# A second chunk pair with seven products in the second and seventh up pairs of each channel mixer

## The chip, the cores and the metric

One core of a Trainium2 chip runs the whole program. The metric is device time in microseconds of one execution; the time given for a kernel is the median of its runs. Engines are named as in the profile: PE is TensorE, DVE is VectorE, ACT is ScalarE, POOL is GpSimd, SP is the queue that issues most loads.

## What is computed

A decoder trunk of two layers over 256 tokens of width 2048, in float32. Layer 0 mixes tokens with gated linear attention, layer 1 with forgetting attention; both also attend to 256 memory tokens. After each mixer comes the channel mixer, which the change touches:

```python
def causal_dwconv(u, w, b):                     # width 3, along the tokens
    up = jnp.pad(u, ((0, 0), (CONV_WIDTH - 1, 0), (0, 0)))
    return w[0] * up[:, 0:s_] + w[1] * up[:, 1:s_ + 1] + w[2] * up[:, 2:s_ + 2] + b

def conv_ffn(h, w_up, conv_w, conv_b, w_down):  # FFN_HIDDEN = 5632
    u = causal_dwconv(h @ w_up, conv_w, conv_b)
    a, val = split_cols(u, [FFN_HIDDEN, FFN_HIDDEN])
    return (jax.nn.silu(a) * val) @ w_down
...
    h = rmsnorm(x, norm_ffn[i])
    x = x + conv_ffn(h, ffn_w_up[i], ffn_conv_w[i], ffn_conv_b[i], ffn_w_down[i])
```

## The kernel before

**Products in parts.** Weights come from memory in float32, in units of 128 rows by up to 1024 columns. Each unit is split: ScalarE casts it to the matmul's shorter format (`whi`), VectorE subtracts that from the original (`wlo`). Activations are held in the same two parts. A product then takes three matmuls: high by high, low by high, high by low.

**The channel mixer.** Its 44 hidden blocks of 128 channels are worked through in groups of four, called up pairs here and named by their first block j = 0, 4, 8, ... 40: eleven a layer. One up pair multiplies all 256 tokens (two blocks of 128) by 1024 columns, in 16 chunks of 128 rows of the weights, one unit each. For an ordinary chunk there are four products (two token blocks by two column halves), twelve matmuls of 128 x 512. Blocks 0 to 15, 16 to 31 and 32 to 43 form three parts (`PARTS`). After the up pairs of a part and one pair of the next, two `down_pair` calls multiply the finished blocks by the down weights. So pairs 0, 4, 8, 12, 16 come first, then two down pairs, then 20, 24, 28, 32, two down pairs, 36, 40, and the rest of the down projection.

**Seven products.** `pair_steps` can take two neighbouring chunks as the two halves of a 2 x 2 block product, with seven products instead of eight: 21 matmuls instead of 24. For that it needs sums of the activations (a tile `usum` or `dsum`, made by `input_sums` and `token_sums`) and sums of the weights, which VectorE makes in place (L425 to L428). It also splits four pieces where two chunks need two:

```python
w1 = split_more(ra[:, :512], 512)
w2 = split_more(rb, 1024)
# four differences on VectorE, L425 to L428, over ra and rb
w3 = split_more(ra, 1024)
w4 = split_more(rb, 1024)
```

`raw2` has two buffers, so a second such chunk pair in one up pair loads its units once the first pair's are used up. Eight banks gather the products. When the last chunk pair of seven is done, `early` combines four of them, on ScalarE (L1464, L1465, L1471) and VectorE (L1466 to L1469); at the end of the up pair `late` (L1475) adds the others. Before the change every up pair has chunks 6 and 7 taken so (`SEVEN_UP`), and pairs 20 and 36, the first after each two down pairs, have chunks 11 and 12 as well (`SEVEN_MORE`).

**Convolution.** An up pair's results are transposed on VectorE (L1427), sent to memory and back by GpSimd's queue, and then become taps on ScalarE (L1376), tap sums on VectorE (L1383), a silu (L1389) and a gated product (L1396, L513, L514). `drive` gives this work out chunk by chunk during the next up pair, from its eighth chunk on, and it runs on into the pair behind that.

**Order.** A scheduler fixes each engine's order of instructions when the program is built; splits have a raised priority, and taps are tied behind the last cast issued. Buffers `raw`, `whi` and `wlo` are four deep, so weights are split about three chunks ahead.

Of the kernel before, what the change touches and what calls it, by code (L numbers as in the profile page):

```python
# [35 lines left out]
SEVEN_DOWN = (4, 10)  # L36
SEVEN_MORE = 11
# [108 lines left out]
def _trunk(ctx: ExitStack, tc: tile.TileContext, xt, xtok, memt, wp, wgu, gns, gfin, cnv, par, msk, out):  # L146
# [310 lines left out]
    def token_sums(r, dst):  # L457

        t = r.rearrange("p s (b n) -> p (s b) n", b=2)
        a11, a21, a12, a22 = (t[:, n, :] for n in range(4))  # L460
        V.tensor_tensor(a22, a21, a22, ALU.add)
        V.tensor_tensor(a21, a11, a21, ALU.subtract)
        V.tensor_tensor(a11, a22, a11, ALU.subtract)
        V.tensor_tensor(a12, a12, a11, ALU.subtract)
        halves([dst[:, part] for part in range(2)], t)
# [846 lines left out]
    def down_pair(l, p, f, src, sums, flip, pool, temps, then=None):  # L1312

        def early(bank):
            t0, t1 = temps()
            S.activation(t0, bank["p1"], AF.Copy)
            add_to(f)(0, t0)
            V.tensor_tensor(t0, bank["p6"], t0, ALU.add)
            V.tensor_tensor(t1, bank["p7"], t0, ALU.add)
            add_to(f)(1, t1)  # L1320
            add_to(f + 1)(1, t1)
            add_to(f + 1)(1, bank["p5"])
            V.tensor_tensor(t0, bank["p5"], t0, ALU.add)
            add_to(f + 1)(0, t0)

        def late(b, h, a):
            add_to(f + h)(b, a)
            if then is not None:
                then(f + h, b)

        return pair_steps(where["down", l, p, f], src, sums, flip, pool, early, late)
# [26 lines left out]
    def ffn(l, nx, h, m, ys, zs, landing, then, pool, temps, last=None, spare=None):  # L1358
        with tc.tile_pool(name=f"ffn{l}", bufs=1) as fp:
# [8 lines left out]
            def held(name, i):  # L1368
                return fp.tile([P, 2, 4, P], F32R, name=name, tag=f"{name}{i}")
# [36 lines left out]
            def input_sums(k, tag="usum", at=None):  # L1406

                r = fp.tile([P, 2, T], F32, name="cv", tag="cv")
                for s in range(2):
                    V.tensor_tensor(r[:, s, :], h[k + s][:, 0, :].bitcast(F32), h[k + s][:, 1, :].bitcast(F32), ALU.add)  # L1410
                t = held(tag, k if at is None else at)
                token_sums(r, t)
                return t
# [42 lines left out]
            def up_pair(j, more={}):  # L1456

                count[2] += 1
                turns = [turn(j + 2 * h_, 8) for h_ in range(2)]
                u = {}  # L1460

                def early(bank):
                    u.update({(b, h_): temps(2 * b + h_) for b in range(2) for h_ in range(2)})
                    S.activation(u[0, 1], bank["p1"], AF.Copy)  # L1464
                    S.activation(u[0, 0], bank["p1"], AF.Copy, scale=scale(0))  # L1465
                    V.tensor_tensor(u[0, 1], bank["p6"], u[0, 1], ALU.add)  # L1466
                    V.tensor_tensor(u[1, 0], bank["p7"], u[0, 1], ALU.add)
                    V.tensor_tensor(u[0, 1], bank["p5"], u[0, 1], ALU.add)
                    V.tensor_tensor(u[1, 1], bank["p5"], u[1, 0], ALU.add)  # L1469
                    for b, h_ in ((0, 1), (1, 0), (1, 1)):  # L1470
                        S.activation(u[b, h_], u[b, h_], AF.Copy, scale=scale(b))  # L1471

                def late(b, h_, a):
                    with tc.issue_after(turned_last[0].ins) if h_ and not b else nullcontext():
                        V.scalar_tensor_tensor(u[b, h_], a, scale(b), u[b, h_], ALU.mult, ALU.add)  # L1475
                    turns[h_](b, u[b, h_])

                return pair_steps(where["up", l, j], h, {**up_sums, **more}, count[2] % 2, pool, early, late)
# [6 lines left out]
            def drive(steps, share=1.3):  # L1485
                for _ in steps:
                    tick(share)
# [2 lines left out]
            for k in up_pair(0):  # L1490
                first(k)
            done = 4
            more = {}
            for p, (lo, hi) in enumerate(PARTS[:-1]):
                while done < hi + 4:
                    drive(up_pair(done, more))
                    more = {}
                    done += 4
                src = [m[c % RING] for c in range(lo, hi)]
                for f in (0, 2):  # L1500
                    count[2] += 1
                    drive(down_pair(l, p, f, src, {c - lo: t for c, t in sums.items() if f}, count[2] % 2, pool,
                                    lambda: (temps(0), temps(1))))
                sums.clear()
                more = {SEVEN_MORE: input_sums(SEVEN_MORE, "dsum", SEVEN_DOWN[0])}
            lo, hi = PARTS[-1]
            while done < hi:
                drive(up_pair(done, more), 1.3 if done + 4 < hi else 1.7)
                more = {}
                done += 4  # L1510
            p = len(PARTS) - 1
# [83 lines left out]
    with tc.tile_pool(name="stash", bufs=1) as st:  # L1595
        vt = st.tile([P, 2, FOX_H * HD], F32, name="fvt")
        turned3 = vt.rearrange("p b t -> p (b t)").rearrange("p (f q k b j) -> p f q k b j", f=3, q=4, k=4, b=2)
        turned3 = [turned3[:, f] for f in range(3)]

        with tc.tile_pool(name="turn1", bufs=1) as tp:  # L1600
            n2, then = preparing("kv", bufB, tp, dram, turned3, "raw2", nc.gpsimd)
            ys = [const.tile([P, 4, 4, 2, 32], F32, name="yu", tag=tag) for tag in ("mk0", "mv0")]
            fixed = [vt.rearrange("p b t -> p (b t)")[:, 2048 + 512 * i : 2560 + 512 * i] for i in range(2)]

            def temps(i):
                return fixed[i] if i < 2 else tp.tile([P, 512], F32, name="temp", tag=f"temp{i}")

            more = []
            for t, tag in ((mk, "mk1"), (mv, "mv1")):
                parked.append(dram.tile([P, 4 * T], F32, name="park" + tag, tag="park" + tag, bufs=1))  # L1610
                nc.gpsimd.dma_start(parked[-1], t[1].rearrange("p a b -> p (a b)"))
                more.append(const.tile([P, 2, 2, T], F32R, name="more" + tag, tag=tag))
            ffn(0, n, bufB, bufA + [t[:, i] for t in more for i in range(2)], ys, turned3, ys, then, tp, temps)
        fox(n2, vt, turned3)
# [9 lines left out]
    with tc.tile_pool(name="store", bufs=1) as op:  # L1624
# [55 lines left out]
        then.begin = begin  # L1680
        more = [op.tile([P, 2, T], F32R, name=f"more{i}") for i in range(RING - KC)]
        ffn(1, n, bufA, bufB + more, ys, zs, zs, then, op, temps, last, spare)


# [69 lines left out]
```

## Time and profile before

| | |
|---|---|
| three timed runs | 2239.08, 2239.31, 2239.30 us; median 2239.3 us |
| the profiled execution | 2237.85 us |
| its span, first to last instruction | 2236.1 us |
| granted TensorE clock, mean | 0.997 |
| matmuls | 10323 |

Busy time of an engine is given in microseconds and as a share of the span. Idle time stands in brackets or behind a bar, with the engine or transfer that ended it. A group names line, engine and operation, then out<-in by tile names.

### The profile page before, as it was taken

To read this page: it belongs to the slowest core of one execution; us is meant where nothing else is said; L and a number is where in the kernel's file an instruction comes from. 1 tells how busy PE (TensorE), PEld (TensorE's weight loads), DVE (VectorE), ACT (ScalarE), POOL (GpSimd) and SP (SyncE) were. 2 spreads that over 40 slices of the span, in tenths; PEclk is the share of its full clock that TensorE was granted. 3 is DMA by queue.
4 is the path that set the end of the run, shared out by engine and by line. 5 is a ranking of instruction groups with operands and counts; after the bars stand their busy time and mean duration, and the time that the engine had idled before them with its cause. 6 is when DMAs were issued, how large, how long until landed. Compare 5 with 4: busy or idle time off the path is not lost.

```text
span 2236.1 us, 30039 instructions
## 1 busy us (share of the span) xinstructions
PE 2212.4 (99%) x10323; PEld 1853.4 (83%) x10323; DVE 1781.5 (80%) x2638; ACT 1419.7 (63%) x2255; POOL 137.2 (6%) x259
## 2 busy tenths in 40 slices
PE   9999999999999999999999999999999999999998
PEld 7888888888788888888877998888878888888886
DVE  7768977688887889888868559668898788978876
ACT  6655664556786567665665455455787647676466
POOL 0000000001100001100111000000100000110010
PEclk9999999999999999999999999999999999999999
DMA  9867567777677567766677767777677756765674
GB/s 347 252 220 226 195 187 245 245 244 240 216 248 251 197 212 254 228 220 215 229 245 252 217 199 247 221 243 240 222 231 240 246 196 233 259 231 208 223 240 160
DMA packets 165633, 515.47 MB, mean 231 GB/s; under 512 B 20700, under 2 KB 41832, under 8 KB 165480
## 3 DMA queue, kind: packets, MB, share of 16 engines
q1 hardware_dynamic: 148200, 460.32, 62.1%
q0 software_dynamic: 16704, 52.44, 7.6%
q8 instruction: 81, 1.33, 0.2%
q10 hardware_dynamic: 576, 0.79, 0.1%
q14 instruction: 72, 0.59, 0.1%
HBM read 469.68 MB, written 43.79 MB: 230 GB/s over the span
## 4 chain that ended last, share of the span: by engine, by line
PE 91%; ACT 4%; issue 2%; DMA 2%; DVE 0%; POOL 0%; SPq 0%; ACTq 0%; DVEq 0%; POOLq 0%
PE acc L400 27%; PE acc L333 24%; PE ps_s L400 14%; PE ps_o L400 7%; PE ps_t L400 7%; PE acc L305 3%; PE acc L260 3%; PE ps_s L333 2%; ACT tap L1376 2%; PE acc L258 1%; DMA fvt<-far 1%; ACT whi L229 1%; PE acc L361 1%; DMA yzu<-far 1%; PE ps_s L1007 0%
## 5 line engine op out<-in xcount | busy, mean ns | idle before, releaser
L230 DVE TENSOR_TENSOR wlo<-raw,whi 128x1024 fp32r<-128x1024 f32 (+4 forms) x739 | 874.9, 1195 | 296.7 <-ACT whi L229 270.2
L229 ACT ACTIVATE whi<-raw 128x1024 fp32r<-128x1024 f32 (+4 forms) x739 | 761.4, 1037 | 448.2 <-PE acc L333 165.8
L333 PE MATMUL acc<-whi,B 128*128 128x512 f32 (+3 forms) x1248 | 294.9, 371 | 8.7 <-ACT B L524 8.7
L333 PEld LDWEIGHTS acc<-whi,B 128*128 128x128 f32 x1248 | 228.1, 189 | 37.5 <-ACT B L524 9.1
L375 ACT ACTIVATE whi<-raw 128x1024 fp32r<-128x1024 f32 (+1 forms) x136 | 129.8, 955 | 196.6 <-PE acc L400 78.3
L400 PE MATMUL acc<-whi,B 128*128 128x512 f32 x794 | 203.3, 390 | 1.4 <-ACT whi L229 1.3
L376 DVE TENSOR_TENSOR wlo<-raw,whi 128x1024 fp32r<-128x1024 f32 (+1 forms) x136 | 148.0, 1089 | 71.0 <-ACT whi L375 62.4
L400 PE MATMUL acc<-whi,mix 128*128 128x512 f32 x754 | 192.6, 390 | 0.9 <-ACT whi L229 0.7
L400 PEld LDWEIGHTS acc<-whi,B 128*128 128x128 f32 x794 | 148.5, 188 | 34.6 <-ACT whi L229 3.8
L400 PEld LDWEIGHTS acc<-whi,mix 128*128 128x128 f32 x754 | 141.3, 188 | 32.3 <-ACT whi L229 2.6
L333 PE MATMUL acc<-wlo,B 128*128 128x512 f32 (+3 forms) x624 | 159.8, 370 | 0.0
L1376 ACT ACTIVATE tap<-yzu,cw 128x256 f32<-128x256 f32 x264 | 124.5, 530 | 6.2 <-DMA yzu<-far 6.0
L1376 ACT ACTIVATE tap<-fvt,cw 128x256 f32<-128x256 f32 x264 | 124.4, 530 | 4.9 <-DMA fvt<-far 4.9
L333 PEld LDWEIGHTS acc<-wlo,B 128*128 128x128 f32 x624 | 114.9, 188 | 14.6
L1383 DVE TENSOR_TENSOR tap<-tap,tap 128x1024 f32<-128x1024 f32 x88 | 106.9, 1214 | 18.8 <-ACT tap L1376 18.8
L400 PE MATMUL acc<-wlo,B 128*128 128x512 f32 x397 | 112.3, 390 | 0.0
L400 PE MATMUL ps_s<-whi,mix 128*128 128x512 f32 x394 | 107.3, 389 | 0.0
L400 PE MATMUL acc<-wlo,mix 128*128 128x512 f32 x377 | 106.6, 390 | 0.0
L400 PE MATMUL ps_s<-whi,B 128*128 128x512 f32 x342 | 94.2, 389 | 0.0
L400 PEld LDWEIGHTS acc<-wlo,B 128*128 128x128 f32 x397 | 74.4, 188 | 15.9 <-DVE wlo L230 0.5
L400 PEld LDWEIGHTS ps_s<-whi,mix 128*128 128x128 f32 x394 | 74.0, 188 | 15.7
L400 PEld LDWEIGHTS acc<-wlo,mix 128*128 128x128 f32 x377 | 70.6, 188 | 15.2 <-DVE wlo L230 0.5
(490 smaller groups left out, 3756.0 us busy)
## 6 DMA issues: line engine op xcount, KB each, us to landing
raw<-wp SPq DMA_DIRECT2D x743, 512.0 KB, 4.5
fvt<-far POOLq DMA_DIRECT2D x100, 128.0 KB, 5.4
raw<-wp SPq DMA_DIRECT2D x32, 384.0 KB, 3.4
far<-yu POOLq DMA_DIRECT2D x22, 512.0 KB, 5.6
far<-yzu POOLq DMA_DIRECT2D x22, 512.0 KB, 5.8
yzu<-far POOLq DMA_DIRECT2D x88, 128.0 KB, 5.0
raw<-wp SPq DMA_DIRECT2D x24, 388.0 KB, 3.7
x<-xtok SPq DMA_DIRECT2D x8, 512.0 KB, 5.7
```

Of the source, the lines that this page charges most:

```text
L229: casts.append(S.activation(hi[:, s], raw[:, s], AF.Copy))
L230: lows.append(V.tensor_tensor(lo[:, s], raw[:, s], hi[:, s].bitcast(F32), ALU.subtract))
L258: mm = TE.matmul(acc[p][c][:, :T], w[:, s], both[:, 0, :], start=False, stop=end and j == 3)
L260: mm = TE.matmul(acc[p][c], w[:, s], both, start=u == j == 0, stop=end and j == 3)
L305: mm = TE.matmul(acc[b][:, :n], src[kcs[j] - base][:, part, b * P : (b + 1) * P], w, start=u == 0 and low == part == j == 0, stop=u == end ...
L333: mm = TE.matmul(acc[b][:, :n], src[kc - base][:, part, b * P : (b + 1) * P], ready[low][:, j * n : (j + 1) * n], start=i == low == part = ...
L361: mm = TE.matmul(acc[b][:, :n], src[kc - base][:, part, b * P : (b + 1) * P], w, start=i == low == part == j == 0, stop=i == end and low = ...
L375: casts.append(S.activation(hi[:, :n], src, AF.Copy))
L376: lows.append(V.tensor_tensor(lo[:, :n], src, hi[:, :n].bitcast(F32), ALU.subtract))
L400: r = TE.matmul(bank[name], x, w, start=name not in begun, stop=last)
L1376: S.activation(by_run(taps[i][:, s, c, i:]), zs[slot][:, :, 2 * c + s], AF.Copy if i else AF.Identity, bias=0.0 if i else w[3], scale=w[2 ...
L1383: V.tensor_tensor(taps[0], taps[0], taps[n][:, :, :, :T], ALU.add)
```

## The change

`more` names the additional chunk pair of the next up pair. The change makes its sums already after up pair 0, in the tile that block sums number 4 use later (`dsum4`), and lets pair 4 take them. In the second part it keeps them for one pair longer, so that pair 24 has them beside pair 20. Pair 36 is as before. Four up pairs of a layer then take chunks 11 and 12 with seven products instead of two. Lines behind 1493 move down by one.

```diff
             for k in up_pair(0):
                 first(k)
             done = 4
-            more = {}
+            more = {SEVEN_MORE: input_sums(SEVEN_MORE, "dsum", SEVEN_DOWN[0])}
             for p, (lo, hi) in enumerate(PARTS[:-1]):
                 while done < hi + 4:
                     drive(up_pair(done, more))
-                    more = {}
+                    if not p or done != lo + 4:
+                        more = {}
                     done += 4
```

## The prediction

> **What bounds the kernel now.** I read the page's busy times and chain first, then a table of stretches, one per pair of weight panels, then TensorE's waits, then VectorE's queue in order of time.
>
> ```profile
> span 2236.1 us, 30039 instructions
> ...
> PE 2212.4 (99%) x10323; PEld 1853.4 (83%) x10323; DVE 1781.5 (80%) x2638; ACT 1419.7 (63%) x2255; POOL 137.2 (6%) x259
> ...
> PE 91%; ACT 4%; issue 2%; DMA 2%; DVE 0%; POOL 0%; SPq 0%; ACTq 0%; DVEq 0%; POOLq 0%
> ```
>
> TensorE (PE) is the chain: 91% of it. Whatever takes matmuls away pays, as long as nothing makes TensorE wait instead. The profiled execution took 2237.85 us, 1.75 us around its span; the median of the three timed runs, 2239.3 us, is 1.45 us more. I add the change to the span and carry both differences along.
>
> The next rows are whole pairs: up pair 4, up pair 8, up pair 20 (already with two chunk pairs of seven products), up pairs 24 and 28, all of the first layer. Columns: stretch, length, then busy time of PE, weight loads, VectorE (DVE), ScalarE (ACT), GpSimd.
>
> ```profile
> core 0: us, PE busy (x) PEld busy (x) DVE busy (x) ACT busy (x) POOL busy (x), PEclk, DMA share, GB/s
> 500.50:543.40 42.90, 42.90 (x190) 35.46 (x189) 33.81 (x39) 31.83 (x50) 5.44 (x10) 1.00 0.72 233
> 543.40:587.20 43.80, 43.41 (x190) 35.32 (x189) 38.42 (x49) 33.48 (x54) 5.47 (x10) 1.00 0.70 234
> 760.00:802.40 42.40, 42.40 (x187) 34.92 (x186) 33.70 (x38) 22.94 (x25) 0.00 (x0) 1.00 0.57 194
> 802.40:845.50 43.10, 43.10 (x190) 35.32 (x189) 34.98 (x43) 32.13 (x51) 5.50 (x10) 1.00 0.72 233
> 845.50:888.60 43.10, 43.10 (x190) 35.38 (x190) 38.44 (x46) 33.02 (x54) 5.47 (x10) 1.00 0.76 244
> ```
>
> Pair 20 gives the pace: 42.40 / 187 = 0.227 us a matmul. It runs without a wait because the down pairs ahead of it left no convolution work: ScalarE has 22.94 us to do. Pairs 4 and 24, which the change edits, carry 31.83 and 32.13. Only pairs 8, 24 and 28 here make TensorE wait, and they wait for splits of weights:
>
> ```profile
> PEld acc L400 <- ACT whi L229: 0.5, 2, 0.2
> PEld ps_o L400 <- ACT whi L229: 0.2, 1, 0.2
> ...
> PEld acc L400 <- ACT whi L229: 0.8, 1, 0.8
> PEld acc L400 <- DVE wlo L230: 0.3, 1, 0.3
> ```
>
> The first two lines are pairs 24 and 28 together, the last two pairs 4 and 8. So the slack behind TensorE is nearly spent there, and the quarters of pair 24 and the first of pair 28 show where:
>
> ```profile
> 813.10:823.80 10.70, 10.70 (x48) 8.63 (x47) 5.21 (x7) 6.43 (x11) 2.17 (x4) 1.00 0.59 155
> 823.80:834.50 10.70, 10.70 (x48) 8.72 (x48) 10.50 (x11) 10.70 (x18) 0.00 (x0) 1.00 0.53 177
> 834.50:845.40 10.90, 10.90 (x50) 9.03 (x49) 9.53 (x15) 10.81 (x21) 0.00 (x0) 1.00 0.79 263
> 845.50:856.20 10.70, 10.70 (x49) 8.83 (x48) 10.70 (x14) 4.98 (x7) 2.66 (x5) 1.00 0.88 326
> ```
>
> VectorE idles half of the second quarter and then hardly at all. The idle quarter cannot be borrowed: the convolution's taps, which feed the later sums, come back from memory only at its end.
>
> ```profile
> 820.28 2.52 ACT L1376 ACTIVATE tap<-fvt,cw 128x256 f32<-128x256 f32 x6 [0.90 <-DMA fvt<-far]
> ```
>
> **The change part by part.** *Matmuls.* In four pairs (4 and 24 of both layers) chunks 11 and 12 take 7 x 3 products instead of 2 x 12: 12 matmuls fewer in all, 12 x 0.227 = 2.7 us, on the path. The Trainium skill, "TensorE: Matmul & The Clock Gate", section "Wait — 56ns, not 53.3ns?", gives 215.7 ns for a warm matmul of 512; by that estimate the saving would be 2.6 us, and the row's 227 ns decides.
>
> *Splits.* Instead of two casts and two low parts there are four of each, one of them half as wide, and four differences (L425 to L428) on VectorE.
>
> ```profile
> L376 DVE TENSOR_TENSOR wlo<-raw,whi 128x1024 fp32r<-128x1024 f32 x15 | 18.4, 1224 | 9.6 <-ACT whi L375 9.4
> L427 DVE TENSOR_TENSOR raw<-raw,raw 128x512 f32<-128x512 f32 x5 | 3.5, 691 | 0.1
> L376 DVE TENSOR_TENSOR wlo<-raw,whi 128x512 fp32r<-128x512 f32 x5 | 3.4, 687 | 2.3 <-PE ps_t L400 1.4 <-ACT whi L375 1.0
> L375 ACT ACTIVATE whi<-raw 128x1024 fp32r<-128x1024 f32 x15 | 15.9, 1061 | 21.2 <-PE ps_t L400 11.2 <-PE acc L400 7.5 <-DVE raw L426 2.4
> L375 ACT ACTIVATE whi<-raw 128x512 fp32r<-128x512 f32 x5 | 3.2, 634 | 6.9 <-PE ps_t L400 3.3 <-PE acc L400 1.7 <-DVE wlo L230 1.6
> ```
>
> Added per pair: 2 x 1.22 of low parts less the two replaced, so one wide, one half (1.22 + 0.69) and 4 x 0.69, 4.7 us of VectorE; neighbours overlap a little (two low parts take 2.35 us in a row quoted below, not 2.44), so 4.5 us of its queue. ScalarE gets 1.06 + 0.63 = 1.7 us, and new waits: its third and fourth casts want VectorE's differences. Behind them stand the early sums and the casts of chunks 13 and 14, and TensorE waits for all three.
>
> *Moved.* The early sums of products (L1464 to L1469) follow the last chunk pair of seven, so they go from chunk 6 to chunk 11, behind the second split and before the convolution's second half. *Loads.* The second chunk pair's two loads wait on SP for the first's buffers, with the later weight loads queued behind them. In pair 20 this is already so:
>
> ```profile
> 775.54 3.04 SPq L419 DMA_DIRECT2D raw<-wp  x2
> ...
> raw<-wp SPq DMA_DIRECT2D x743, 512.0 KB, 4.5
> ```
>
> They go out 15.5 to 18.6 us into a pair and land 4.5 us later, by 23.1; TensorE needs them after 129 matmuls, at 29. I count nothing; were the cover gone, they would cost what they are late. GpSimd's queue keeps its order. *Input sums.* Once a layer, during pair 0: seven more VectorE steps, none wider than 512, so at most 7 x 0.69 = 4.8 us. Pair 0's last quarter has 10.80 - 5.71 = 5.1 us free, so I count nothing; with that cover gone it would cost up to those 4.8 us a layer.
>
> ```profile
> 489.60:500.40 10.80, 10.80 (x49) 8.97 (x48) 5.71 (x6) 3.83 (x4) 0.00 (x0) 1.00 0.77 254
> ```
>
> **VectorE's queue from pair 24 into pair 28.** The built program shows the new order. From the first tap sum (L1383) to the last split of pair 28's own seven products it holds what it held, plus 4.5 us, plus the four early sums (4 x 0.6, 0.69 less the overlap; before they ran ahead of it). The old stretch and its idle time:
>
> ```profile
> 830.15 1.22 DVE L1383 TENSOR_TENSOR tap<-tap,tap 128x1024 f32<-128x1024 f32 x1
> 831.29 2.35 DVE L230 TENSOR_TENSOR wlo<-raw,whi 128x1024 fp32r<-128x1024 f32 x2
> ...
> 838.20 1.23 DVE L230 TENSOR_TENSOR wlo<-raw,whi 128x1024 fp32r<-128x1024 f32 x1 [0.55 <-ACT whi L229]
> 839.95 1.23 DVE L230 TENSOR_TENSOR wlo<-raw,whi 128x1024 fp32r<-128x1024 f32 x1 [0.52 <-ACT whi L229]
> ...
> 843.02 1.23 DVE L230 TENSOR_TENSOR wlo<-raw,whi 128x1024 fp32r<-128x1024 f32 x1 [0.19 <-ACT whi L229]
> ...
> 865.35 1.23 DVE L376 TENSOR_TENSOR wlo<-raw,whi 128x1024 fp32r<-128x1024 f32 x1 [1.66 <-ACT whi L375]
> ```
>
> It ran from 830.15 to 866.6, 36.4 us with 2.9 idle: 33.5 of work. With 6.9 more and all idle gone it is 40.4; it starts about 1.1 sooner, the early sums no longer being ahead of it, so it ends at 829.05 + 40.4 = 869.5, 2.9 us later than before. TensorE needs that last split at once, so it is late by as much, though it has 0.7 us less to do. One 0.2 us wait after it goes, since casts now stand ahead of taps: net +2.7 us. The floor comes from whole stretches (823.8 on is chunk 8's low part):
>
> ```profile
> 823.80:866.60 42.80, 39.51 (x50) 1.00 0.72 240
> 1877.90:1921.20 43.30, 39.62 (x50) 1.00 0.69 240
> 520.80:564.30 43.50, 37.96 (x45) 1.00 0.69 233
> 1576.20:1619.00 42.80, 37.97 (x45) 1.00 0.69 234
> ```
>
> 39.51 + 4.5 = 44.0 does not fit into 42.80: at least +1.2. If all idle stays, +4.5. In the second layer the same stretch has room for 0.4 more: +2.2 (0.8 to 4.5). Pairs 4 and 8 have more slack: 37.96 + 4.5 is 1.0 below the first room and, in the second layer, 37.97 + 4.5 is 0.3 below. Laid out the same way the queue ends 1.1 later there, since the new splits wait for each other, but pair 8's old wait of 0.8, for a cast behind eight taps, goes, because casts move ahead of them: I take +0.3, and +0.9 in the second layer, where the room is 0.7 smaller (each from -1.0, the saving and that wait in part, to +4.0).
>
> Sum, the saving inside each term: 2.7 + 2.2 + 0.3 + 0.9 = 6.1, rounded to +6.0 us. Span 2242.1, profiled time 2243.9, median 2245.3 us. Without the saving the waits would be 8.7.
>
> **The rivals.** *The saving holds (not slower).* The convolution work slips behind without TensorE noticing: its results are wanted only by a down pair much later. For: pair 20 has two chunk pairs and no wait. Against: low parts stand in the same queue as tap sums, and 44.0 does not fit 42.8. It decides if the queue lets splits pass. 2239.3 - 2.7 = 2236.6; chance 0.12. *Idle time all used.* Each stretch at its floor: 1.2 + 0.8 in pairs 24 and 28, -0.7 each in 4 and 8, where only the saving is left: +0.6, 2239.9; chance 0.24. *ScalarE ties the knot.* In pairs 8 and 28 the new order puts the early sums' first two ScalarE steps ahead of the third cast, in pair 28 a copy of chunk sums too; the early sums wait for TensorE, and TensorE for the cast. For: VectorE must finish that copy's input first, late as it is. Against: there the old cast waited for VectorE anyway. It decides if the cast starts later than VectorE's second difference allows. Three half-wide ScalarE steps of 0.6 in each following pair, on top of the forecast: 4 x 1.8 = 7.2, 2252.5; chance 0.13. *The clock falls.*
>
> ```profile
> 1173.00:1184.00 11.00, 5.12 (x14) 4.08 (x15) 8.97 (x34) 4.53 (x13) 4.52 (x9) 0.54 1.03 330
> ```
>
> Between the layers TensorE is idle for some 9 us and the granted clock drops to 0.54 for the next stretch; here, if the waits lump into a single long one, about 10 us at half speed costs 5 us more in each of pairs 28: 2255.3; chance 0.03. The Trainium skill's page above, Part 1, lets the clock drop after an idle window of about 3.4 us; the up pairs' waits so far, 0.8 at most, leave it at 1.00, which agrees. That the change does not do what it says is out: the built order shows the new products.
>
> **How the numbers follow.** The forecast has 0.48. The range 2238.0 to 2252.5 leaves out the first rival and the last, 0.15. About 0.2%, 4.5 us, is what a measurement of this kernel can tell from no change. Faster by that, below 2234.8, needs the whole saving and most old waits gone: 0.02, out of the first rival. Within it lie the rest of the first two rivals, 0.34, and 0.02 of the forecast's own low end: 0.36. Slower, above 2243.8: the rest, 0.62.
>
> **What would show it.** Right: 10311 matmuls; pair 24 no shorter than its 43.1, more likely 44; VectorE without idle time from the second split to pair 28's seven; pair 28 some 2 us longer with TensorE waiting for L376 or L375; pair 8 without its old waits. Wrong: pairs 24 and 28 at 42.4 and 43.0, or VectorE idle at 860.

## The result, and the profile after

The changed kernel takes 2251.64 us (median of six runs, 2250.76 to 2254.24), the kernel before, run beside it, 2239.19 us (six runs, 2237.99 to 2241.40). The ratio is 1.0057, 95% interval 1.0047 to 1.0068: 12.4 us slower, twice the +6.0 that was forecast. The profiled execution took 2254.01 us, its span 16.1 us more than that of before. A second profiled execution of the same kernel (below) took 2251.61 us, the median.

The page of the changed kernel:

```profile
span 2252.2 us, 30067 instructions
...
PE 2217.4 (98%) x10311; PEld 1850.3 (82%) x10311; DVE 1798.5 (80%) x2676; ACT 1425.4 (63%) x2265; POOL 137.1 (6%) x259
...
PE 83%; issue 7%; DMA 3%; ACT 3%; DVE 3%; POOL 1%; SPq 0%; ACTq 0%; DVEq 0%; POOLq 0%
```

There are 12 matmuls fewer, as the change promises, and the share of TensorE in the chain falls from 91% to 83%. Most of that went to "issue" (2% to 7%), time for which the profile shows no wait, and the second execution has 89%, so what TensorE waits for is better read from the stretches. The first layer's up pairs 4, 8, 24, 28 and 32 of the changed kernel, as stretches:

```profile
core 0: us, PE busy (x) PEld busy (x) DVE busy (x) ACT busy (x) POOL busy (x), PEclk, DMA share, GB/s
500.30:543.70 43.40, 43.29 (x188) 34.65 (x187) 34.96 (x41) 29.26 (x44) 5.45 (x10) 1.00 0.67 215
543.70:590.20 46.50, 44.76 (x190) 36.40 (x189) 41.00 (x51) 37.18 (x63) 5.46 (x10) 0.96 0.77 245
805.30:848.60 43.30, 43.22 (x187) 34.57 (x186) 34.94 (x41) 28.38 (x43) 5.50 (x10) 1.00 0.68 220
848.60:893.60 45.00, 43.26 (x191) 35.32 (x190) 40.64 (x53) 36.87 (x62) 5.47 (x10) 1.00 0.73 244
893.60:937.60 44.00, 43.55 (x191) 35.28 (x190) 41.13 (x53) 34.92 (x57) 5.46 (x10) 1.00 0.77 244
```

Pairs 4 and 24 (first and third row) are edited, have three matmuls fewer, and still take 43.4 and 43.3 instead of 42.9 and 43.1: each has several short waits, of 0.5 us at most, for casts and low parts. The pair behind each pays most: pair 8 46.5 instead of 43.8, pair 28 45.0 instead of 43.1. VectorE's added work has moved behind: 34.94 in pair 24 is what it was (34.98), pair 28 went from 38.44 to 40.64, and pair 32 from 38.25 to 41.13. TensorE's waits name one cause in pair 8 (first line) and in pair 28 (second line):

```profile
PEld ps_s L400 <- ACT whi L375: 2.2, 1, 2.2
PEld acc L400 <- ACT whi L375: 2.4, 2, 2.2
```

Both are for the third cast of the pair's own chunks 6 and 7 (L375). ScalarE in order of time, in pair 28 before and then after; a bracket holds the idle time ahead and what ended it:

```profile
861.23 1.06 ACT L375 ACTIVATE whi<-raw 128x1024 fp32r<-128x1024 f32 x1 [2.37 <-DVE raw L426]
863.20 0.60 ACT L1464 ACTIVATE fvt<-acc 128x512 f32<-128x512 f32 x1 [0.91 <-PE acc L400]
```

```profile
866.01 0.63 ACT L668 ACTIVATE dsum<-cv 128x512 fp32r<-128x512 f32 x1 [5.43 <-DVE cv L464]
866.95 0.60 ACT L1464 ACTIVATE fvt<-acc 128x512 f32<-128x512 f32 x1 [0.30 <-PE acc L400]
867.44 0.68 ACT L1465 ACTIVATE fvt<-acc,ny 128x512 f32<-128x512 f32 x1
868.01 2.01 ACT L375 ACTIVATE whi<-raw 128x1024 fp32r<-128x1024 f32 x2
```

And VectorE's queue of the changed kernel just before that cast:

```profile
864.49 0.72 DVE L1427 STREAM_TRANSPOSE yu<-fvt 128x512 f32<-128x512 f32 x1
865.12 0.66 DVE L425 TENSOR_TENSOR raw<-raw 128x512 f32<-128x512 f32 x1
865.69 0.29 DVE L464 TENSOR_TENSOR cv<-cv 128x128 f32<-128x128 f32 x1
865.88 0.70 DVE L426 TENSOR_TENSOR raw<-raw,raw 128x512 f32<-128x512 f32 x1
...
869.10 2.36 DVE L376 TENSOR_TENSOR wlo<-raw,whi 128x1024 fp32r<-128x1024 f32 x2
```

Before, the third cast started at 861.23, 15.7 us into the pair and 0.1 behind VectorE's second difference (L426), which it needs. After, it starts at 868.01, 19.4 us into the pair: 3.7 later. The second difference has become late too, it ends at 866.58, 18.0 into the pair, 2.4 later than before. But the cast does not follow it. On ScalarE the two copies for the early sums (L1464, L1465) now stand ahead of the cast, and the first of them waits for one of TensorE's products of the same chunks. Pair 8 shows it better. The second difference ends at 561.57 there, and ScalarE is idle, but it stays so until the copy can start at 562.00:

```profile
562.00 0.60 ACT L1464 ACTIVATE fvt<-ps_o 128x512 f32<-128x512 f32 x1 [2.12 <-PE ps_o L400]
562.49 0.68 ACT L1465 ACTIVATE fvt<-ps_o,ny 128x512 f32<-128x512 f32 x1
563.06 2.00 ACT L375 ACTIVATE whi<-raw 128x1024 fp32r<-128x1024 f32 x2
```

In pairs 8 and 28 of both layers, and in both executions, the cast starts 19.4 us into the pair, while the second difference ends anywhere between 17.5 and 18.4, and TensorE waits 2.1 us each time. So this wait is made of the two copies and the cast, one behind the other after TensorE's own product. VectorE's lateness lies inside it; the run with the differences on GpSimd (e8, below) takes the two apart.

Pair 8 lost more than its 2.2 us, and the granted clock shows why:

```profile
565.50:568.90 3.40, 3.40 (x10) 2.62 (x9) 3.40 (x4) 3.40 (x6) 0.47 (x1) 0.50 0.61 206
```

From 1.3 us behind the wait TensorE had half its clock for 3.4 us; by these numbers about 1.7 us were lost.

### The profile page after: what moved, and what is told of

The parts are those of the page before. It is cut to its first block, busy times and chain, and to the rows that moved or that the text cites. A ratio compares the mean times of both kernels' runs of the same rounds, so it can differ in the third digit from the quotient of the medians.

```text
span 2252.2 us, 30067 instructions
## 1 busy us (share of the span) xinstructions
PE 2217.4 (98%) x10311; PEld 1850.3 (82%) x10311; DVE 1798.5 (80%) x2676; ACT 1425.4 (63%) x2265; POOL 137.1 (6%) x259
## 4 chain that ended last, share of the span: by engine, by line
PE 83%; issue 7%; DMA 3%; ACT 3%; DVE 3%; POOL 1%; SPq 0%; ACTq 0%; DVEq 0%; POOLq 0%
PE acc L400 25%; PE acc L333 23%; PE ps_s L400 12%; PE ps_o L400 6%; PE ps_t L400 6%; PE acc L305 3%; PE acc L260 3%; PE ps_s L333 2%; PE acc L258 1%; ACT tap L1376 1%; DMA raw<-wp 1%; DMA yzu<-far 1%; ACT whi L229 1%; DMA far<-blk 1%; PE acc L361 1%
## 5 line engine op out<-in xcount | busy, mean ns | idle before, releaser
L230 DVE TENSOR_TENSOR wlo<-raw,whi 128x1024 fp32r<-128x1024 f32 (+4 forms) x731 | 866.1, 1196 | 294.8 <-ACT whi L229 274.8
L229 ACT ACTIVATE whi<-raw 128x1024 fp32r<-128x1024 f32 (+4 forms) x731 | 751.7, 1037 | 440.0 <-PE acc L333 156.1
L375 ACT ACTIVATE whi<-raw 128x1024 fp32r<-128x1024 f32 (+1 forms) x152 | 144.1, 953 | 206.0 <-PE acc L400 77.9
L376 DVE TENSOR_TENSOR wlo<-raw,whi 128x1024 fp32r<-128x1024 f32 (+1 forms) x152 | 164.9, 1089 | 70.8 <-ACT whi L375 63.5
L400 PEld LDWEIGHTS acc<-wlo,B 128*128 128x128 f32 x392 | 73.3, 188 | 16.1 <-DVE wlo L230 0.9
```

Of the source, the lines that this page charges most:

```text
L229: casts.append(S.activation(hi[:, s], raw[:, s], AF.Copy))
L230: lows.append(V.tensor_tensor(lo[:, s], raw[:, s], hi[:, s].bitcast(F32), ALU.subtract))
L375: casts.append(S.activation(hi[:, :n], src, AF.Copy))
L376: lows.append(V.tensor_tensor(lo[:, :n], src, hi[:, :n].bitcast(F32), ALU.subtract))
L400: r = TE.matmul(bank[name], x, w, start=name not in begun, stop=last)
```

## The experiments

Each kernel was timed in five rounds beside the kernel before, except the last, which is one profiled execution. The table gives what its trace has over the trace of before, in us, taken from the first weight load of each stretch to that of the next; both layers are added up. "Between" is the stretch from the last block of the first layer's channel mixer to the second layer's pair 0 (356.2 us before).

| kernel | pairs 4, 24 | pairs 8, 28 | pairs 12, 16, 32 | pair 0 | pairs 20, 36 | between | span | median, ratio [95%] |
|---|---|---|---|---|---|---|---|---|
| changed | +3.8 | +7.8 | +0.7 | +0.9 | 0.0 | +2.4 | +16.1 | 2251.64, 1.0057 [1.0047, 1.0068] |
| changed, again | +4.2 | +6.2 | +0.9 | +0.2 | 0.0 | +1.5 | +13.7 | 2251.61, one execution |
| e1 pair 4 only | +1.8 | +3.9 | -0.4 | 0.0 | 0.0 | +1.3 | +7.1 | 2244.57, 1.0019 [1.0010, 1.0027] |
| e2 pair 24 only | +1.7 | +5.9 | +1.4 | +0.8 | 0.0 | +4.0 | +16.0 | 2251.24, 1.0048 [1.0036, 1.0061] |
| e3 early copies behind casts | +1.2 | +8.0 | -1.7 | +0.2 | 0.0 | +3.1 | +11.1 | 2248.28, 1.0036 [1.0022, 1.0049] |
| e4 the same, on before | +0.7 | -0.1 | -2.6 | +0.1 | 0.0 | +3.8 | +1.5 | 2239.04, 0.9997 [0.9988, 1.0006] |
| e5 second layer only | +0.9 | +5.4 | +0.2 | +0.2 | 0.0 | +1.1 | +7.9 | 2245.96, 1.003 [1.002, 1.004] |
| e6 differences left out | -2.3 | +1.3 | +0.6 | 0.0 | 0.0 | +3.0 | +2.3 | 2242.65, 1.0010 [1.0002, 1.0019] |
| e7 chunks 2, 3 | +8.9 | +0.1 | -0.4 | +0.9 | +0.1 | +4.1 | +13.7 | 2252.59, 1.0059 [1.0046, 1.0073] |
| e8 differences on GpSimd | +15.0 | +6.2 | -0.4 | +0.2 | 0.0 | +4.1 | +27.0 | 2264.09, 1.0113 [1.0099, 1.0126] |
| e9 chunks 1, 2 | +9.8 | 0.0 | +0.4 | 0.0 | +0.2 | -0.6 | +8.6 | 2248.46, 1.0047 [1.0035, 1.0060] |
| e10 chunks 0, 1 | -2.3 | +0.4 | 0.0 | +1.6 | +5.9 | -0.8 | +6.4 | 2241.41, 1.0015 [1.0006, 1.0024] |
| e11 chunks 0, 1 in 4, 24 | -0.2 | +1.0 | 0.0 | +1.0 | 0.0 | +1.2 | +2.6 | 2242.04, 1.0009 [1.0000, 1.0018] |

The kernel before had medians of 2237.87 to 2240.01 beside these; the ratios use the one of the same chip. A trace is one execution and can lie off the median of its row: that of the changed kernel took 2.4 us more, e2's 2.6 and e10's 2.9 more, e6's 2.4 and e9's 2.0 less. Pair 40, the down pairs and the two ends of the program are not listed and make up the rest of each span.

**One half at a time.** Against the changed kernel, e1 clears `more` after every pair, and e2 has no sums after pair 0:

```diff
-                    if not p or done != lo + 4:
-                        more = {}
+                    more = {}
```

```diff
-            more = {SEVEN_MORE: input_sums(SEVEN_MORE, "dsum", SEVEN_DOWN[0])}
+            more = {}
```

> Only pair 4 of each layer takes chunks 11 and 12 with seven products besides pairs 20 and 36; pair 24 is as before. Theory A (VectorE's queue is in arrears after a double pair) and theory B (in the pair behind it ScalarE's early copy, which waits for TensorE, stands ahead of the third cast) both put the cost into pairs 4 and 8: from the two traces +0.4 and +1.1 us a layer, 1.7 more where the clock falls, so 2241 to 2244 us. Theory C (the cost is the scheduler's new order elsewhere, 2.4 us between the layers) expects that 2.4 us here too, and nothing more.

> Only pair 24 of each layer takes the second chunk pair; pair 4 is as before and no input sums are made during pair 0. A and B: pairs 24 and 28, +0.3 and +1.8 in the first layer, +0.6 and +1.9 in the second without the late taps, so 2243 to 2246 us, and more than for pair 4 alone. C: no more than for pair 4 alone; the two kernels' costs don't add up to the 12.4 us of both.

Measured: +4.6 us and +11.2 us of median; e2 is 5 us above what was expected of it. Each half pays mostly in the pair behind the edited one, and there the third cast stands behind the copies again and starts 19.4 us into the pair or later, so the halves act by the same mechanism. Their sum, 15.8, is more than the whole change costs. e2's trace has +4.0 between the layers and 3.4 us at half clock in the second layer's pair 28, which is part of the excess in that execution; what makes up the rest of its median is not shown.

**ScalarE's order.** In `early`, the two copies are tied behind the last cast, in the changed kernel (e3) and in the kernel before (e4):

```diff
+                    with tc.issue_after(casts[-1].ins):
+                        S.activation(u[0, 1], bank["p1"], AF.Copy)
+                        S.activation(u[0, 0], bank["p1"], AF.Copy, scale=scale(0))
-                    S.activation(u[0, 1], bank["p1"], AF.Copy)
-                    S.activation(u[0, 0], bank["p1"], AF.Copy, scale=scale(0))
```

> The changed kernel, with the early sums' two ScalarE steps tied behind the fourth cast of the chunk pair. B: the third cast starts as soon as VectorE's second difference is there, 1.4 us sooner in pair 28 and 1.4 in pair 8, so the four waits of 2.1 us fall to about 0.7 and the total by 4 x 1.4 = 5.6 us and the fall of the clock goes: 2244 to 2247 us. A: VectorE ends its queue no sooner, the low parts are late by as much: 2249 to 2252 us.

> The kernel before, with the same tie. B: its fourth cast stood behind the same early steps (VectorE idles 1.66 and 2.03 us for it), but TensorE waited little there: 2237 to 2239.5 us. A: no change, 2239.

Measured: 2248.28 us, between the two theories' ranges: 8.3 above the kernel before beside it, where the changed kernel was 12.4 above. The gain does not come from pairs 8 and 28, which keep +8.0 (3.4 us at half clock are in this number and in the changed kernel's +7.8). ScalarE of e3 in its pair 28:

```profile
863.11 1.06 ACT L375 ACTIVATE whi<-raw 128x1024 fp32r<-128x1024 f32 x1 [0.78 <-DVE raw L426]
864.83 0.72 ACT L513 ACTIVATE mix<-cv 128x256 fp32r<-128x256 f32 x2 [0.66 <-DVE cv L1396]
866.65 1.06 ACT L375 ACTIVATE whi<-raw 128x1024 fp32r<-128x1024 f32 x1 [1.09 <-DVE raw L428]
```

The copies are out of the way, the third cast starts 0.1 us behind the second difference, and the casts wait for VectorE's differences instead. TensorE's waits there:

```profile
PEld acc L400 <- ACT whi L375: 1.8, 2, 1.5
PEld acc L400 <- DVE wlo L376: 1.0, 1, 1.0
```

So the order on ScalarE set the wait of the changed kernel, and with it gone VectorE's late differences cost about as much: the two lie over each other and do not add up. What e3 gains stands in pairs 4 and 24 (+1.2 instead of +3.8 and +4.2) and in pairs 12, 16 and 32; in the latter e4 gains as much (-2.6) without the change. e4's median is level with before; its trace loses 3.8 us between the layers. The tie also lets the scheduler order VectorE anew, so e3 is no pure test of the copies.

**VectorE's added work.** e6 leaves the four differences (L425 to L428) out wherever the second chunk pair is taken. Lines behind them stand one lower.

```diff
+                    if k != SEVEN_MORE:
                         V.tensor_tensor(ra[:, :512], ra[:, 512:], ra[:, :512], ALU.subtract)
...
```

> The four differences of the second chunk pair (L425 to L428) are left out of the changed kernel, in pairs 20 and 36 too, so part of the result is not computed. VectorE's queue has 4 x 0.69 = 2.8 us less to do in each pair with two chunk pairs, ScalarE's order is as it was. If VectorE's arrears make pairs 8 and 28 wait, the waits of 2.1 us there go to nothing and the kernel takes 2243 to 2246. If the early copies ahead of the third cast on ScalarE make them, a wait of 1.4 us or more stays in each and the kernel takes 2249 to 2251.

Measured: 2242.65 us. With 2.8 us less of VectorE a pair, pairs 4 and 24 are 0.5 to 0.7 shorter than before, the saving whole; pair 8 is 0.4 to 0.7 shorter, pair 28 1.2 longer. TensorE's waits in e6's pair 28 no longer hold one of 2 us:

```profile
PEld ps_o L400 <- ACT whi L229: 1.0, 2, 0.8
PEld acc L400 <- DVE wlo L376: 0.7, 1, 0.7
PEld acc L400 <- ACT whi L375: 0.2, 1, 0.2
```

One statement of the expectation was wrong: ScalarE's order did not stay. With the differences gone the scheduler put the third cast ahead of the copies again, as e6's pair 28 shows (L1465 is the copy here):

```profile
860.14 1.06 ACT L375 ACTIVATE whi<-raw 128x1024 fp32r<-128x1024 f32 x1
861.44 0.60 ACT L1465 ACTIVATE fvt<-acc 128x512 f32<-128x512 f32 x1 [0.23 <-PE acc L400]
```

So with the differences both reasons went at once. The run shows that the added differences bring the waits of 2.1 us, and not which of the two reasons makes them.

**The place of the work.** The number is 2 in e7, 1 in e9 and 0 in e10, in pairs 20 and 36 too; the early sums then follow chunk 7 again.

```diff
-SEVEN_MORE = 11
+SEVEN_MORE = 2
```

> The changed kernel with the second chunk pair at chunks 2 and 3 instead of 11 and 12, in all pairs that have one. The early sums then follow chunk 7 as before, and VectorE's idle second quarter takes the added splits. If the place of the added work is what costs, the waits of pairs 8 and 28 go back to those of before, 0.8 and 0.2 us, four pairs keep 0.7 us each, and the kernel takes 2236.5 to 2240, plus whatever the order between the layers adds (up to 4 us). If the amount of VectorE's and ScalarE's work costs wherever it stands, pairs 8 and 28 keep about 2 us each: 2248 or more.

Measured: pairs 8 and 28 are back (+0.1 in all) with all of the added work still there, and the third cast of both stands ahead of the copies again, as it does in e9, e10 and e11. So it was the place, behind the taps and with the early sums moved, that made them wait. But pairs 4 and 24 now lose 2.1 to 2.4 us each. ScalarE in e7's pair 4:

```profile
514.12 0.63 ACT L375 ACTIVATE whi<-raw 128x512 fp32r<-128x512 f32 x1 [2.18 <-DMA raw<-wp]
516.83 2.01 ACT L375 ACTIVATE whi<-raw 128x1024 fp32r<-128x1024 f32 x2 [2.09 <-DMA raw<-wp]
```

The units of chunks 6 and 7 come late, for their loads wait for the two buffers that chunks 2 and 3 hold.

> The changed kernel with the second chunk pair at chunks 1 and 2. With it at chunks 2 and 3 the waits of pairs 8 and 28 were gone, but the loads of chunks 6 and 7, which wait for the two buffers that chunks 2 and 3 leave, came 2 us late, and pairs 4 and 24 took 2.1 to 2.4 us longer. One chunk earlier the buffers come free up to 2.7 us sooner. If late loads are the whole of it, pairs 4 and 24 drop to -0.7 to +0.3 against before, pairs 8 and 28 stay at -0.5 and +0.6, and the kernel takes 2239 to 2244, of which 1 to 4 us lie between the layers. If VectorE's work at the start of the pair is it, pairs 4 and 24 keep 2 us: 2250 or more.

> The changed kernel with the second chunk pair at chunks 0 and 1, two chunks earlier than in the run at chunks 2 and 3. The loads of chunks 6 and 7 then have 5.4 us more, so if late loads were the whole cost, pairs 4 and 24 are 0.7 us shorter than before and the kernel takes 2236 to 2241 with what lies between the layers. Against it: the four splits and differences of chunks 0 and 1 then fall into the last quarter of the pair ahead, where VectorE ends that pair's sums and transposes (10.7 of 10.7 us busy in the first quarter of pair 28). If that is in the way, pairs 0, 4, 20, 24 or 36 wait 1 to 3 us each at their start: 2245 to 2255.

Measured: at chunks 1 and 2 pairs 4 and 24 still lose 2.0 to 3.1 us, each with a wait of 1.7 for an ordinary cast (L229), which stands behind taps and the copies on ScalarE. The loads of chunks 6 and 7 come late here as well (ScalarE idles 4.8 us for one in pair 4); what each of the two costs was not taken apart. At chunks 0 and 1 they lose nothing. Pairs 20, 24 and 28 of e10:

```profile
760.10:804.00 43.90, 42.73 (x188) 34.80 (x187) 35.15 (x40) 22.29 (x25) 0.00 (x0) 1.00 0.56 191
804.00:846.40 42.40, 42.40 (x188) 34.91 (x187) 36.62 (x45) 34.34 (x53) 5.47 (x10) 1.00 0.76 243
846.40:889.70 43.30, 43.30 (x191) 35.23 (x190) 38.53 (x46) 32.64 (x53) 5.48 (x10) 1.00 0.71 235
```

Pair 24 takes 42.40, without a wait: this is the saving whole, 0.7 us. Three of the four casts of its chunks 0 and 1 run ahead of it, at the end of pair 20, which has no convolution work. The price moved to pairs 20 and 36, which come straight behind down pairs and wait 1.6 us for a cast (L375) at their start, and the second layer's pair 0 waits as long.

**A version without that price.** e11 takes chunks 0 and 1 in pairs 4 and 24 and leaves pairs 20 and 36 as before:

```diff
-            more = {SEVEN_MORE: input_sums(SEVEN_MORE, "dsum", SEVEN_DOWN[0])}
+            more, again = {0: input_sums(0, "dsum", SEVEN_DOWN[0])}, {}
...
-                    if not p or done != lo + 4:
-                        more = {}
+                    more, again = again, {}
...
+                if not p:
+                    again = {0: input_sums(0, "dsum", SEVEN_DOWN[1])}
```

> The second chunk pair at chunks 0 and 1 in pairs 4 and 24 only, where it left no wait when all four pairs had it there; pairs 20 and 36, which waited 1.5 us each with it, keep theirs at chunks 11 and 12 as before. Pairs 4 and 24 should be 0.5 to 0.7 us shorter than before, pairs 8 and 28 stay within 0.2, pairs 20 and 36 go back to 42.4: all up pairs together some 2 us shorter than before, 2236.5 to 2239 if the stretch between the layers is as before, up to 4 us more if it is not. If the added work costs wherever it stands, pairs 4, 8, 24 and 28 are longer by 1 us or more each: 2241 or more.

Measured: 2242.04 us. Pair 4 keeps its saving (-0.6 and -0.5), but pair 24, now behind a pair that has its second chunk pair at chunks 11 and 12, waits at its start:

```profile
PEld ps_t L400 <- ACT whi L375: 1.2, 1, 1.2
```

No version tried beats the kernel before.

**GpSimd.** e8 gives the four differences to GpSimd.

```diff
-                    V.tensor_tensor(ra[:, :512], ra[:, 512:], ra[:, :512], ALU.subtract)
+                    G = nc.gpsimd if k == SEVEN_MORE else V
+                    G.tensor_tensor(ra[:, :512], ra[:, 512:], ra[:, :512], ALU.subtract)
...
```

> The changed kernel with the second chunk pair's four differences on GpSimd instead of VectorE, in pairs 20 and 36 too. GpSimd has 5.5 us to do in such a pair, all of it issuing transfers. If one difference takes it no more than about 1 us, VectorE's relief of 2.8 us shortens the waits of pairs 8 and 28 as far as VectorE makes them: 2244 to 2248. If it takes 2 us or more each, the third and fourth casts wait for it and the pairs with two chunk pairs wait themselves, some 2 to 4 us each: over 2255.

Measured: the worst of all, 2264.09 us. Of GpSimd's groups (one line lower than in the other kernels):

```profile
L429 POOL TENSOR_TENSOR raw<-raw 128x512 f32<-128x512 f32 x8 | 17.1, 2142 | 0.6
L427 POOL TENSOR_TENSOR raw<-raw,raw 128x512 f32<-128x512 f32 x8 | 10.3, 1292 | 0.6
```

A difference takes it 1.3 to 2.1 us where VectorE takes 0.69, and pairs 4 and 24 take 3.1 to 4.1 us longer each (with 3.4 us at half clock in pair 24 of both layers), as the second theory of the expectation has it. Pairs 20 and 36 have such differences too and take no longer.

Pair 28 of e8, which starts at 852.63, is the case that parts the two reasons. First VectorE's second difference for the pair's own chunks, then ScalarE:

```profile
868.33 0.68 DVE L427 TENSOR_TENSOR raw<-raw,raw 128x512 f32<-128x512 f32 x1
...
870.98 0.60 ACT L1465 ACTIVATE fvt<-acc 128x512 f32<-128x512 f32 x1 [1.89 <-PE acc L400]
871.47 0.68 ACT L1466 ACTIVATE fvt<-acc,ny 128x512 f32<-128x512 f32 x1
872.04 2.00 ACT L375 ACTIVATE whi<-raw 128x1024 fp32r<-128x1024 f32 x2
```

VectorE is only 0.8 us later than before: the difference ends 16.4 us into the pair instead of 15.6. ScalarE idles, and still the cast starts 19.4 us into the pair, 3.0 behind its input, and TensorE waits the same 2.1 us. Copies ahead of the cast are enough for this wait. Why the scheduler puts them ahead here and not in e6, which takes the same four instructions off VectorE, no run tells.

**What repeats.** e5 makes the change in the second layer alone; the last run is the changed kernel itself once more.

```diff
-            more = {SEVEN_MORE: input_sums(SEVEN_MORE, "dsum", SEVEN_DOWN[0])}
+            more = {SEVEN_MORE: input_sums(SEVEN_MORE, "dsum", SEVEN_DOWN[0])} if l else {}
...
-                    if not p or done != lo + 4:
+                    if not l or not p or done != lo + 4:
```

> The change in the second layer alone. Two causes for the time lost between the layers, where the code is untouched. If it is what the first layer's new order leaves behind, the stretch between the layers takes 356.2 us as before, the first layer's up pairs stay within 0.3 us each, and only the second layer's pairs pay, some +1.5 in pair 8, +2 in pair 28, up to +1 in pair 0 and in pair 32: about 2244. If any edit of the program moves the scheduler's order there, the stretch is 1 to 4 us longer here too: 2245 to 2248.

> The changed kernel as it is, profiled once more, to see which of its differences come again. What the order of the instructions makes should: waits of 2.1 us in pairs 8 and 28 of both layers, pair 0 of the second layer 0.9 longer. What the transfers of one execution made should not: the taps that came 2.7 us late in the second layer's pair 24 (its +2.8 falls to about +0.5), and the place where the clock halves. The +2.4 between the layers stays within 0.5 if it is the order, and moves by 1 us or more if it is the execution.

Measured: in e5 the first layer's pairs are as before within 0.2 up to pair 36 (pair 40 is 0.6 shorter), TensorE's order there is the same, and the stretch between the layers is 1.1 longer all the same. In the second execution of the changed kernel that stretch is +1.5 instead of +2.4. In e9 the order there is as before too, with -0.6. So 1 to 2 us of any such number can belong to the execution. The larger ones, +3.8 in e4 and +4.1 in e7, go with an altered order of the instructions there; why the scheduler alters it, no run here tells. Pair 0 of the second layer falls from +0.9 to +0.2, which the expectation had put down to the order. The taps that came late in the second layer's pair 24 did so in both executions, by different amounts (the pair's +2.8 falls to +1.3, not to +0.5); first then second:

```profile
1886.99 2.51 ACT L1376 ACTIVATE tap<-yzu,cw 128x256 f32<-128x256 f32 x6 [2.66 <-DMA yzu<-far]
```

```profile
1885.22 2.52 ACT L1376 ACTIVATE tap<-yzu,cw 128x256 f32<-128x256 f32 x6 [1.15 <-DMA yzu<-far]
```

The clock did not halve in any up pair of the second execution. Its pairs 4, 8, 24 and 28:

```profile
500.40:544.40 44.00, 43.49 (x188) 34.44 (x187) 34.87 (x40) 28.99 (x43) 5.47 (x10) 1.00 0.68 214
544.40:589.40 45.00, 43.26 (x190) 35.32 (x189) 39.85 (x49) 36.02 (x62) 5.49 (x10) 1.00 0.75 241
804.50:848.80 44.30, 43.70 (x188) 34.47 (x187) 34.97 (x41) 28.26 (x42) 5.52 (x10) 1.00 0.69 218
848.80:893.80 45.00, 43.26 (x191) 35.34 (x190) 40.46 (x53) 36.77 (x62) 5.49 (x10) 1.00 0.74 240
```

Pairs 8 and 28 take 45.0 each, both at full clock: the waits of 2.1 us belong to the order of the instructions, the halved clock to the single execution.

## Why the prediction was right, and where it was too small

The kernel became slower, as forecast, but by twice as much: 2251.6 us lie close to the upper end of the range, 2252.5. The second execution is the cleaner measure for the parts, having the median's time and no lost clock in the up pairs.

- **Saving: right.** 10311 matmuls; where nothing waits (e10's pair 24), 0.7 us a pair come out.
- **Pairs 24 and 28: near in size, half right in mechanism.** Forecast +2.7 and +2.2 in the two layers; the second execution has +3.1 and +3.2, the first +2.1 and +4.7, where late taps make the second layer's large. Pair 24 was to take no less than 43.1, likely 44: it took 43.3 and 44.3 in the first layer. VectorE's queue did fall behind as worked out: the last split of pair 28's seven ended 67.2 us behind pair 24's start instead of 64.1 (66.2 in the first execution), 3.1 later where 2.9 was forecast. But TensorE did not wait for that split. It waited for the third cast, which ScalarE's order held, so part of the agreement in size is luck. VectorE's convolution work slipped behind, as the first rival has it, but only in part: pair 32, not in the sum, pays 0.8 and 0.4.
- **Pairs 4 and 8: the step that failed.** "Pairs 4 and 8 have more slack" gave +0.3 and +0.9. Measured: +2.3 and +1.8. The step compared VectorE's busy time of a whole stretch with the room in it and took the end of VectorE's queue for what TensorE waits for. TensorE waits for pair 8's third cast, and this starts 19.4 us into the pair, behind the two copies, just as in pair 28: the room on VectorE does not enter. The second difference was no proof of room either, it ended 3.0 us later into the pair than before (17.9 instead of 15.0), more than in pair 28. The old wait of 0.8 went, as forecast; a wait of 2.1 took its place. (The second layer's +2.2 and +0.9 are each 0.1 less than their own working gives, 2.7 - 0.4 and 0.3 + 0.7; nothing hangs on it.)
- **ScalarE ties the knot: this rival came true, by its own sign.** In pairs 8 and 28 the cast starts 1.0 to 1.9 us later than VectorE's second difference allows, and e8 shows that the copies alone suffice. Its 2252.5 is also the forecast nearest to the measured 2251.6. But it was priced on top of the forecast, and the two lie over each other: e3 takes the copies away, and the casts wait as long for VectorE. That the sum comes out so near is therefore partly luck; some 2 us of the measured change lie outside the up pairs, where no forecast had anything.
- **The clock falls: in small.** It was worked out for one long wait in each pair 28. Instead a wait of 2.1 us sufficed, for 3.4 us, once in the first execution. The longest wait of the up pairs before was 1.3 us, in the first layer's pair 40, and not the 0.8 that was read; the clock stayed at 1.00 there too.
- **Loads and input sums at nothing: right for the loads**, and e7 shows the price where they come late, 2.1 to 2.4 us a pair. Pair 0, where the input sums are made, is +0.9 and +0.2 in the second layer's two executions, 0.0 in the first's. e2, which makes no sums there, has +0.8 in the second layer, so the sums are not shown to cost anything.
- **Outside up pairs 0 to 36** the forecast had nothing; the second execution has 2.2 us there, 1.5 of it between the layers, about what one execution differs from the next.

Up pairs 0 to 36 together cost 11.5 us net in the second execution where 6.1 was forecast; 2.9 of the gap is pairs 4 and 8, 1.4 pairs 24 and 28, the rest pairs 0, 12, 16 and 32.

## What to carry to other kernels

Room in a stretch is not room in front of the instruction that is waited for. Follow the one instruction that the bottleneck needs through every queue that it stands in, and see what stands ahead of it there and what that waits for: here a copy that waited for TensorE stood ahead of a cast that TensorE needed. Among the kernels that compute everything, fewer matmuls paid only with the added splits at the first two chunks of a pair, and neither behind a down pair nor behind a pair with added splits of its own at chunks 11 and 12; elsewhere the same work cost about 1 to 3 us a pair, with a different wait named each time. And when two reasons hold the same instruction, taking one away shows the other, and their prices do not add up.

## What was not expected of the hardware

A wait of TensorE far shorter than the 3.4 us for which the clock then halves can cost the clock. In the traces of e1, e2, e5, e7, e8 and the two of the changed kernel there are nineteen waits of 2.1 us or more in the up pairs, and four were followed, within 1.3 us, by 3.41 us at 0.50. In e8 two of 1.9 us were, and in e3 one of 1.4. Within an execution these stretches start on one grid: 565.48 and 1179.88 are 614.40 apart, 180 times 3.4133. The Trainium skill, "TensorE: Matmul & The Clock Gate", Part 1, has a free-running window of 3413 ns, which agrees with the grid, and a clock that falls after an idle window of that length, which does not: waits of 1.4 to 2.8 us were enough. Why the other fifteen waits of 2.1 us did not halve it stays open; some of them lay wholly inside one window of the grid as well.
